# Where the additions to the residual stream stand in VectorE's queue during the gate

## The chip, the cores and the metric

The kernel runs on one core of a Trainium2 chip. The core has a matrix engine (PE, TensorE), three engines for elementwise work (DVE or VectorE, ACT or ScalarE, POOL or GpSimd), and SP (SyncE), which here only issues DMAs. Each engine works through its own queue strictly in the order in which the program was built, and waits on semaphores for what the others have to deliver. The metric is the time of one execution on the device in microseconds (us). The median of three runs of the kernel before is 2712.3 us.

## The reference

One layer of a decoder trunk with float32 inputs, 2048 positions and width 1024. The change lies wholly in the last line.

```python
h = x
a = rms_norm(h, pre_mix_g);  z = a @ w_in            # q, k, v, f, u_sg, v_sg
y = concat(rms_norm(forgetting_attention(q, k, v, f + f_bias)),
           rms_norm(chunked_spatial_gating(u_sg, v_sg, ...)))
h = h + rms_norm(y @ w_out, post_mix_g)
c = rms_norm(h, pre_ffn_g)
ff = square(relu(c @ w_ff1)) @ w_ff2
h = h + rms_norm(ff, post_ffn_g)
gate = sigmoid(h @ ple_gate_w + ple_gate_b)
return h + gate * (p @ ple_w)
```

## The kernel before, in words

The kernel goes through its stages one after the other: projection, attention and spatial gating, output projection, the first feed-forward product (FF1), the second (FF2), and the gate. Every product is computed in three float32r matmuls of split operands (lines 104 to 106, `mm3`), each 128x128 by 128x512. FF1 and FF2 use a seven-product scheme. At the end of FF2, `post` normalises the feed-forward output row by row and stores it to the DRAM tensor `yS`; the residual stream before FF lies in the DRAM tensor `hS`.

The gate works on 16 tiles of 128 positions, each in two halves of 512 columns. What belongs to one tile t:

- `load_h(t)` loads the two halves of `hS` into the tile's place and the two halves of `yS` into temporaries from a pool of three (`tmp`), and adds the one to the other on VectorE (line 1452). The sum is h of the last line of the reference. There are four places for h, used in turn: tile t + 4 takes the place of tile t, and so its load waits for the last reader of tile t.
- `turn_p(t)` and `turn_h(t)` transpose p and h on PE (lines 1459 and 1466); ACT and DVE take the result out of PSUM in two parts (lines 116 and 117, `evac_split`).
- `gate(t, mid)`: for each half, PE makes the product with `ple_w` (p2, 6 matmuls) and with `ple_gate_w` (p1, 24 matmuls). Behind the first half's matmuls PE transposes the next tile (`mid`). Then DVE adds the bias (line 1486), ACT takes the sigmoid (1487), DVE multiplies with p2 (1488), POOL adds h (1489; DVE for the last tile), and SP stores the half (1490).

`load_h(t + 2)` is called ahead of `gate(t)`. The order in which the instructions of an engine come to stand in its queue isn't that of the source: a scheduler orders them by what its own model holds ready. In the kernel before it puts the additions of line 1452 where their data are ready by that model. In the steady part of the gate this is two tiles earlier than the call: the addition for tile t + 4 stands behind the first work on tile t's own outputs.

Names in the rows and pieces below: `lr` (lr1 to lr3) are the three output buffers of the gate, `acc11`, `acc10` and `T_0` the places of h, `tmp` the loaded halves of `yS`, `pf` the eight PSUM banks, `pT`, `hT`, `B`, `w1p`, `L`, `R`, `wg` and `wh` the operands of the gate's matmuls.

Of the kernel before, what the change touches and what calls it, by code (L numbers as in the profile page):

```python
# [12 lines left out]
ALU = mybir.AluOpType  # L13
# [4 lines left out]
P = 128  # L18
# [7 lines left out]
NT = S // P  # L26
# [8 lines left out]
def trunk(ctx, tc, x, p, w_in, f_bias, sg_ln_g, sg_ln_b, sg_w, sg_b, att_out_g, sg_out_g,  # L35
# [8 lines left out]
    sc, ve, po, pe, sy = nc.scalar, nc.vector, nc.gpsimd, nc.tensor, nc.sync  # L44
# [12 lines left out]
    yS = dram.tile([S, D], F32, name="yS")  # L57
# [44 lines left out]
    def mm3(ps, l, r, first, last):  # L102

        pe.matmul(ps, l[0], r[0], start=first, stop=False)  # L104
        pe.matmul(ps, l[0], r[1], start=False, stop=False)  # L105
        pe.matmul(ps, l[1], r[0], start=False, stop=last)  # L106
# [859 lines left out]
    def w1_places(pl):  # L966

        all = pl.tile([P, 3, KC, P], F32, name="w1raw")
        return all, [all[:, e] for e in range(3)]
# [4 lines left out]
    _, w1raw = w1_places(w1q)  # L974
# [24 lines left out]
    def new_ps():  # L999
        nonlocal nps  # L1000
        nps += 1
        if pf2 is None or nps % 8 < 3:
            return pf1.tile([P, 512], F32, name="pf1")
        return pf2.tile([P, 512], F32, name="pf2")

    def new_tmp():
        return tmp.tile([P, 512], F32, name="tmp")
# [422 lines left out]
    hts, hT, hplaces = {}, [], []  # L1430
# [13 lines left out]
    def load_h(t):  # L1444

        hts[t] = hplaces[t % 4]
        for hf in range(2):
            hs = slice(hf * 512, (hf + 1) * 512)
            sy.dma_start(hts[t][hf], hS[t * P:(t + 1) * P, hs])
            y = new_tmp()  # L1450
            sy.dma_start(y, yS[t * P:(t + 1) * P, hs])
            ve.tensor_tensor(hts[t][hf], hts[t][hf], y, ALU.add)

    def turn_p(t):
        pt = LR[0][:, t % 2 * PLE:(t % 2 + 1) * PLE]
        sy.dma_start(pt, p[t * P:(t + 1) * P])
        ps = new_ps().rearrange("p (a b) -> p a b", b=P)
        for kc in range(2):
            pe.transpose(ps[:, kc], pt[:, kc * P:(kc + 1) * P], ident)
        evac_split(pTs[:, t % 2], ps[:, :2], 1.0)  # L1460

    def turn_h(t):
        for g in range(2):
            ps = new_ps().rearrange("p (a b) -> p a b", b=P)
            for kk in range(4):
                pe.transpose(ps[:, kk], hts[t][g][:, kk * P:(kk + 1) * P], ident)
            evac_split(hT[2 * (t % 2) + g].rearrange("p h (k c) -> p h k c", k=4), ps, 1.0)

    def gate(t, mid):
        pT = pTs[:, t % 2]  # L1470
        for hf in range(2):
            hs = slice(hf * 512, (hf + 1) * 512)
            p2 = new_ps()
            for kc in range(2):
                w = wple[hf][kc]
                mm3(p2, (pT[:, 0, kc], pT[:, 1, kc]), (w[:, 0], w[:, 1]), kc == 0, kc == 1)
            p1 = new_ps()
            for kc in range(KC):
                w = wgt[hf][kc]
                x = hT[2 * (t % 2) + kc // 4]  # L1480
                cs = slice(kc % 4 * P, kc % 4 * P + P)
                mm3(p1, (x[:, 0, cs], x[:, 1, cs]), (w[:, 0], w[:, 1]), kc == 0, kc == KC - 1)
            if hf == 0 and t + 1 < NT:
                mid()
            ot = LR[1 + (2 * t + hf) % 3]
            ve.tensor_tensor(ot, p1, gb[hf], ALU.add)  # L1486
            sc.activation(ot, ot, AF.Sigmoid)
            ve.tensor_tensor(ot, p2, ot, ALU.mult)  # L1488
            (ve if t == NT - 1 else po).tensor_tensor(ot, ot, hts[t][hf], ALU.add)  # L1489
            sy.dma_start(out[t * P:(t + 1) * P, hs], ot)  # L1490

    wgt = [[], []]

# [7 lines left out]
    last = len(steps2)  # L1501
    early_g = {}

    def at(i, f):
        early_g.setdefault(i, []).append(f)

    for e in range(4):
        kc, hf = e // 2, e % 2
# [25 lines left out]
    gb = []  # L1534
    at(last - 12, late_places)
    for t in range(2):
        at(last - 10 + t, lambda t=t: load_h(t))
    at(last - 17, places2)
    for e in range(6):
        at(last - 17 + 2 * e, lambda e=e: wg_in(wgpl[6 + e]))  # L1540
# [35 lines left out]
    while raws_w:  # L1576
        split_wide()
    for t in range(NT):
        if t + 2 < NT:
            load_h(t + 2)  # L1580
        def turns():
            turn_p(t + 1)
            turn_h(t + 1)

        gate(t, turns)
        for _ in range(2):
            if tail:
                tail.pop(0)()
# [25 lines left out]
```

## Time and profile before

| | |
|---|---|
| runs | 2712.3 us median of 3 (2711.87 to 2718.76) |
| the profiled execution's own time | 2715.74 us |
| its span, first to last instruction | 2714.0 us |
| PE, busy share of the span | 97% |
| DVE, ACT, POOL | 67%, 49%, 30% |
| mean granted TensorE clock | 0.987 of full speed |
| HBM traffic | 173 GB/s over the span |

How to read it: the profile is of one execution, and the times in rows are from the start of its span. A row of the timeline is an instruction with its start, its duration, its engine, line and operands, and in brackets how long its engine had been idle before it and what ended that. Neighbouring instructions of a kind are merged into one row (x2). PE's matmuls are pipelined: one that shows 0.39 us lets the next begin 0.23 us after its own start, so PE's pace is read from starts. The gate begins at about 2460 us and is the last tenth of the span.

### The profile page before, as it was taken

To read this page: it belongs to the slowest core of one execution; us is meant where nothing else is said; L and a number is where in the kernel's file an instruction comes from. 1 tells how busy PE (TensorE), PEld (TensorE's weight loads), DVE (VectorE), ACT (ScalarE), POOL (GpSimd) and SP (SyncE) were. 2 spreads that over 40 slices of the span, in tenths; PEclk is the share of its full clock that TensorE was granted. 3 is DMA by queue.
4 is the path that set the end of the run, shared out by engine and by line. 5 is a ranking of instruction groups with operands and counts; after the bars stand their busy time and mean duration, and the time that the engine had idled before them with its cause. 6 is when DMAs were issued, how large, how long until landed. Compare 5 with 4: busy or idle time off the path is not lost.

```text
span 2714.0 us, 37423 instructions
## 1 busy us (share of the span) xinstructions
PE 2620.9 (97%) x12316; PEld 2127.5 (78%) x12316; DVE 1822.2 (67%) x3212; ACT 1342.5 (49%) x2632; POOL 806.6 (30%) x695
## 2 busy tenths in 40 slices
PE   8999999999899999979999999999999999999998
PEld 7787978777677777757788788888888888888777
DVE  5547586866777655578878677678786696874333
ACT  6344433357777777655555455445435444452111
POOL 5444443410000000243444223336360262401111
PEclk8999999999999999989999999999999999999999
DMA  5565756597878776455655854448466644683331
GB/s 167 143 188 143 197 141 170 149 221 207 199 180 186 165 192 152 134 163 192 218 201 174 305 176 145 150 151 282 139 204 210 199 146 141 208 263 101 105 109 50
DMA packets 440611, 472.85 MB, mean 174 GB/s; under 512 B 155616, under 2 KB 269664, under 8 KB 440416
## 3 DMA queue, kind: packets, MB, share of 16 engines
q1 hardware_dynamic: 430179, 454.39, 56.9%
q10 hardware_dynamic: 10237, 16.07, 2.2%
q8 instruction: 97, 1.59, 0.3%
q14 instruction: 98, 0.80, 0.1%
HBM read 336.38 MB, written 133.96 MB: 173 GB/s over the span
## 4 chain that ended last, share of the span: by engine, by line
PE 46%; DMA 4%; DVE 4%; POOL 2%; issue 2%; ACT 1%; SPq 0%; DVEq 0%; POOLq 0%; ACTq 0%
PE pf L106 15%; PE pf L104 15%; PE pf L105 15%; DMA acc<-hS 2%; POOL lr L1489 1%; DMA w1raw<-in_w_ff_dram 1%; DVE lr L1486 1%; DVE lr L1488 1%; DVE w1p L994 0%; DMA px<-hS 0%; DMA T<-hS 0%; DMA B<-jS 0%; DVE ws L1170 0%; POOL hq L1197 0%; DMA cS<-px 0%
## 5 line engine op out<-in xcount | busy, mean ns | idle before, releaser
L104 PE MATMUL pf<-B,w1p 128*128 128x512 f32 x752 | 298.5, 397 | 14.8 <-ACT w1p L991 13.6
L106 PE MATMUL pf<-B,w1p 128*128 128x512 f32 x752 | 296.5, 394 | 2.8 <-DVE w1p L994 2.7
L1197 POOL TENSOR_TENSOR hq<-hq,hq 128x512 f32<-128x512 f32 x128 | 197.5, 1554 | 336.4 <-ACT hq L1191 298.7
L105 PE MATMUL pf<-B,w1p 128*128 128x512 f32 x752 | 297.3, 395 | 0.0
L660 DVE TENSOR_TENSOR hl<-pr,hl 128x512 fp32r<-128x512 f32 (+1 forms) x320 | 191.9, 608 | 104.6 <-ACT hl L659 87.9
L100 POOL TENSOR_TENSOR wsp<-wraw,wsp 128x344 fp32r<-128x344 f32 (+1 forms) x176 | 199.2, 1149 | 195.1 <-ACT wsp L96 184.6
L651 ACT ACTIVATE pr<-pS,bias 128x512 f32<-128x512 f32 (+1 forms) x320 | 196.6, 622 | 108.8 <-PE pS L647 66.2
L172 DVE TENSOR_REDUCE mx<-pM 128x1 f32<-128x512 f32 (+3 forms) x288 | 169.5, 597 | 78.4 <-PE pM L169 77.7
L104 PEld LDWEIGHTS pf<-B,w1p 128*128 128x128 f32 x752 | 141.8, 189 | 49.6 <-ACT w1p L991 14.1
L104 PE MATMUL pacc<-wsp,wide 128*128 128x344 f32 (+1 forms) x480 | 167.6, 349 | 8.8 <-ACT ug L358 5.5
L104 PE MATMUL pf<-R,L 128*128 128x512 f32 x452 | 175.9, 389 | 0.0
L105 PE MATMUL pf<-R,L 128*128 128x512 f32 x452 | 175.8, 389 | 0.0
L106 PE MATMUL pf<-R,L 128*128 128x512 f32 x452 | 175.8, 389 | 0.0
L106 PEld LDWEIGHTS pf<-B,w1p 128*128 128x128 f32 x752 | 141.6, 188 | 37.4 <-DVE w1p L994 4.3
L105 PEld LDWEIGHTS pf<-B,w1p 128*128 128x128 f32 x752 | 141.8, 189 | 31.9
L106 PE MATMUL pacc<-wsp,wide 128*128 128x344 f32 (+1 forms) x480 | 163.4, 340 | 0.5 <-DVE wide L117 0.5
L105 PE MATMUL pacc<-wsp,wide 128*128 128x344 f32 (+1 forms) x480 | 163.2, 340 | 0.0
L659 ACT CAST hl<-pr 128x512 fp32r<-128x512 f32 (+3 forms) x272 | 146.5, 549 | 8.6 <-DMA vS<-hl 2.2
L991 ACT CAST L<-lr 128x512 fp32r<-128x512 f32 x113 | 70.3, 622 | 150.1 <-PE pf L105 120.1
L994 DVE TENSOR_TENSOR w1p<-ws,w1p 128x512 fp32r<-128x512 f32 (+1 forms) x136 | 117.2, 867 | 36.7 <-ACT w1p L991 35.2
L994 DVE TENSOR_TENSOR L<-lr,L 128x512 fp32r<-128x512 f32 x113 | 96.0, 849 | 64.8 <-ACT L L991 64.6
L991 ACT CAST w1p<-w1raw 128x512 fp32r<-128x512 f32 (+1 forms) x123 | 73.4, 598 | 128.7 <-PE pf L105 121.9
(443 smaller groups left out, 7187.1 us busy)
## 6 DMA issues: line engine op xcount, KB each, us to landing
hidC<-hq SPq DMA_DIRECT2D x224, 256.0 KB
lr<-hidC SPq DMA_DIRECT2D x224, 256.0 KB
w1raw<-in_w_ff_dram SPq DMA_DIRECT2D x64, 512.0 KB
w1raw<-in_w_ff_dram SPq DMA_DIRECT2D x128, 256.0 KB
wraw<-in_w_in_dram SPq DMA_DIRECT2D x96, 256.0 KB
wraw<-in_w_in_dram SPq DMA_DIRECT2D x88, 172.0 KB
KM<-kS ACTq DMA_DIRECT2D x80, 132.0 KB
jS<-C SPq DMA_DIRECT2D x19, 512.0 KB
```

The costliest lines, as they stand in the source:

```text
L100: e.tensor_tensor(dst[:, 1], src, dst[:, 0].bitcast(F32), ALU.subtract)
L104: pe.matmul(ps, l[0], r[0], start=first, stop=False)
L105: pe.matmul(ps, l[0], r[1], start=False, stop=False)
L106: pe.matmul(ps, l[1], r[0], start=False, stop=last)
L172: ve.tensor_reduce(mx[:, tt, c:c + 1], ps[:, :full], AX.X, ALU.max)
L651: sc.activation(pr[:, off:], ps[:, off:], AF.Exp, bias=bias_of(b)[:, j, h:h + 1])
L659: sc.copy(hl[:, 0, off:], pr[:, off:])
L660: ve.tensor_tensor(hl[:, 1, off:], pr[:, off:], hl[:, 0, off:].bitcast(F32), ALU.subtract)
L991: sc.copy(dst[:, 0], src)
L994: (po if lo == "pool" else ve).tensor_tensor(dst[:, 1], src, dst[:, 0].bitcast(F32), ALU.subtract)
L1197: po.tensor_tensor(t, x, y, op)
L1486: ve.tensor_tensor(ot, p1, gb[hf], ALU.add)
```

## The change

`load_h` keeps its loads and returns a function that does the two additions. In the gate's loop this function is called behind `gate(t)`, within a block that queues what it traces on VectorE behind one given instruction: the tile's last multiplication (line 1488 before, 1492 now). Such an edge sets the order in VectorE's queue alone; nothing waits for it. For tiles 0 and 1, which are loaded during FF2, the additions follow their loads as before.

```diff
     def load_h(t):
         hts[t] = hplaces[t % 4]
+        ys = [new_tmp() for _ in range(2)]
         for hf in range(2):
             hs = slice(hf * 512, (hf + 1) * 512)
             sy.dma_start(hts[t][hf], hS[t * P:(t + 1) * P, hs])
-            y = new_tmp()
-            sy.dma_start(y, yS[t * P:(t + 1) * P, hs])
-            ve.tensor_tensor(hts[t][hf], hts[t][hf], y, ALU.add)
+            sy.dma_start(ys[hf], yS[t * P:(t + 1) * P, hs])
+
+        def add_h():
+            for hf in range(2):
+                ve.tensor_tensor(hts[t][hf], hts[t][hf], ys[hf], ALU.add)
+        return add_h
...
-            ve.tensor_tensor(ot, p2, ot, ALU.mult)
+            done = ve.tensor_tensor(ot, p2, ot, ALU.mult)
             (ve if t == NT - 1 else po).tensor_tensor(ot, ot, hts[t][hf], ALU.add)
             sy.dma_start(out[t * P:(t + 1) * P, hs], ot)
+        return done
...
-        at(last - 10 + t, lambda t=t: load_h(t))
+        at(last - 10 + t, lambda t=t: load_h(t)())
...
     for t in range(NT):
-        if t + 2 < NT:
-            load_h(t + 2)
+        add_h = load_h(t + 2) if t + 2 < NT else None
...
-        gate(t, turns)
+        done = gate(t, turns)
+        if add_h is not None:
+            with tc.issue_after(done.ins):
+                add_h()
```

The order of PE's, ACT's and POOL's instructions stays what it was. DVE's queue in the gate, before, for tile 1 (its halves go to lr3 and lr1; acc11_2 and acc11_3 are the place of tile 5):

```order
L1486 TENSOR_TENSOR lr3_15928<-pf2_22557,acc10_0_17919 128x512
L117 SCALAR_TENSOR_TENSOR pT4_17928<-pf2_22583,pT4_17928 128x256
L117 SCALAR_TENSOR_TENSOR hT0_22082<-pf2_22588,hT0_22082 128x512
L117 SCALAR_TENSOR_TENSOR hT1_22083<-pf2_22595,hT1_22083 128x512
L1488 TENSOR_TENSOR lr3_15928<-pf2_22550,lr3_15928 128x512
L1452 TENSOR_TENSOR acc11_2_17925<-acc11_2_17925,tmp_22769 128x512
L1486 TENSOR_TENSOR lr1_15926<-pf1_22614,acc10_1_17920 128x512
L1488 TENSOR_TENSOR lr1_15926<-pf1_22607,lr1_15926 128x512
L1452 TENSOR_TENSOR acc11_3_17926<-acc11_3_17926,tmp_22773 128x512
L1486 TENSOR_TENSOR lr2_15927<-pf2_22681,acc10_0_17919 128x512
```

The same place now (T_0 is the place of tile 3):

```order
L1490 TENSOR_TENSOR lr3_15928<-pf2_22555,acc10_0_17919 128x512
L117 SCALAR_TENSOR_TENSOR pT4_17928<-pf2_22581,pT4_17928 128x256
L117 SCALAR_TENSOR_TENSOR hT0_22082<-pf2_22586,hT0_22082 128x512
L117 SCALAR_TENSOR_TENSOR hT1_22083<-pf2_22593,hT1_22083 128x512
L1492 TENSOR_TENSOR lr3_15928<-pf2_22548,lr3_15928 128x512
L1490 TENSOR_TENSOR lr1_15926<-pf1_22612,acc10_1_17920 128x512
L1492 TENSOR_TENSOR lr1_15926<-pf1_22605,lr1_15926 128x512
L1455 TENSOR_TENSOR T_0_15924<-T_0_15924,tmp_22542 128x512
L1455 TENSOR_TENSOR T_0_15924<-T_0_15924,tmp_22543 128x512
L1490 TENSOR_TENSOR lr2_15927<-pf2_22679,acc10_0_17919 128x512
```

Before, one addition for the tile four ahead stood behind each half; now both additions for the tile two ahead stand behind the second half. The four additions for tiles 2 and 3 thereby leave DVE's queue in the last steps of FF2.

SP's queue before, from the store of tile 1's first half on (tmp_22875 is a half of tile 6, tmp_22973 of tile 7):

```order
L1490 DMA out_0_dram<-lr3_15928 128x512
L1449 DMA acc11_2_17925<-hS_62 128x512
L1451 DMA tmp_22875<-yS_63 128x512
L1490 DMA out_0_dram<-lr1_15926 128x512
L1449 DMA acc11_3_17926<-hS_62 128x512
L1451 DMA tmp_22973<-yS_63 128x512
```

The same place now (tmp_22667 is the second half of tile 4, tmp_22768 the first of tile 5):

```order
L1494 DMA out_0_dram<-lr3_15928 128x512
L1450 DMA acc11_2_17925<-hS_62 128x512
L1494 DMA out_0_dram<-lr1_15926 128x512
L1451 DMA tmp_22667<-yS_63 128x512
L1451 DMA tmp_22768<-yS_63 128x512
L1450 DMA acc11_3_17926<-hS_62 128x512
```

The loads of `hS` keep their place behind the stores; those of `yS` now stand in pairs behind the second half's store, and each fetches for a nearer tile.

## Rows read from the trace of the kernel before

**Rows 1.** The page's head

```profile
span 2714.0 us, 37423 instructions
```

**Rows 2.** Busy time by stretch: length, PE, PEld, DVE, ACT, POOL, clock, DMA

```profile
2420.00:2440.00 20.00, 20.00 (x90) 16.57 (x89) 15.91 (x25) 8.00 (x14) 0.65 (x1) 1.00 0.92 299
...
2467.67:2542.00 74.33, 74.33 (x351) 61.48 (x350) 26.98 (x46) 14.20 (x25) 12.15 (x10) 1.00 0.37 119
2542.00:2671.23 129.23, 123.26 (x561) 98.80 (x560) 44.51 (x74) 20.93 (x41) 21.90 (x17) 0.99 0.32 100
...
2553.40:2556.80 3.40, 3.40 (x8) 2.64 (x9) 0.54 (x1) 0.00 (x0) 1.28 (x1) 0.53 0.25 92
...
2671.23:2707.92 36.69, 36.69 (x171) 30.08 (x169) 10.74 (x17) 5.88 (x11) 5.14 (x4) 1.00 0.10 37
```

**Rows 3.** PE's waits in the gate: who, for whom, us in total, times, longest

```profile
PE pf L106 <- DVE pT L117: 5.2, 6, 1.7
PE pf L104 <- DVE lr L1488: 0.6, 1, 0.6
```

**Rows 4.** PE's timeline: start, us; the transposes of p, one row a tile

```profile
2467.67 0.38 PE L1459 MATMUL pf<-ident,lr 128*128 128x128 f32 x2
...
2542.00 0.38 PE L1459 MATMUL pf<-ident,lr 128*128 128x128 f32 x2
...
2671.23 0.38 PE L1459 MATMUL pf<-ident,lr 128*128 128x128 f32 x2
...
2686.10 0.38 PE L1459 MATMUL pf<-ident,lr 128*128 128x128 f32 x2
```

**Rows 5.** PE's timeline at its first long wait in the gate

```profile
2552.21 0.50 PE L106 MATMUL pf<-B,pT 128*128 128x512 f32 x1 [1.67 <-DVE pT L117]
...
2553.40 0.63 PE L104 MATMUL pf<-wg,hT 128*128 128x512 f32 x1
...
2556.39 0.63 PE L105 MATMUL pf<-wg,hT 128*128 128x512 f32 x1
```

**Rows 6.** DVE's waits in the gate

```profile
DVE acc L1452 <- DMA acc<-hS: 89.1, 18, 5.8
DVE T L1452 <- DMA T<-hS: 24.2, 5, 4.9
```

**Rows 7.** The chain that ended last, in order of time: start, us, what

```profile
2482.05 3.27 DMA acc<-hS
...
2488.91 1.30 POOL lr L1489
...
2490.61 3.03 DMA acc<-hS
...
2498.14 2.84 DMA acc<-hS
...
2546.50 3.93 DMA acc<-hS
...
2627.34 2.81 DMA acc<-hS
```

**Rows 8.** Line 1452's additions in the gate: ns min/median/max, first and last start

```profile
L1452 DVE TENSOR_TENSOR acc<-acc,tmp x18: 691/693/695, 2479.0 to 2647.1; 128x512 f32<-128x512 f32 x18
L1452 DVE TENSOR_TENSOR T<-T,tmp x6: 691/692/693, 2525.8 to 2662.9; 128x512 f32<-128x512 f32 x6
```

**Rows 9.** The timeline of DVE, POOL and PE in tile 13

```profile
2680.80 0.69 DVE L1488 TENSOR_TENSOR lr<-pf,lr 128x512 f32<-128x512 f32 x1 [0.70 <-ACT lr L1487]
...
2681.57 1.28 POOL L1489 TENSOR_TENSOR lr<-lr,acc 128x512 f32<-128x512 f32 x1 [5.54 <-DVE lr L1488]
...
2686.32 0.93 PE L1466 MATMUL pf<-ident,T 128*128 128x128 f32 x7
```

**Rows 10.** The timeline of POOL and DVE near the end of FF2

```profile
2421.03 0.65 POOL L993 TENSOR_SCALAR wh<-tmp 128x512 fp32r<-128x512 f32 x1 [14.83 <-DMA tmp<-in_ple_gate_w_dram]
...
2421.11 1.10 DVE L994 TENSOR_TENSOR w1p<-w1raw,w1p 128x512 fp32r<-128x512 f32 x1
```

## The prediction

> **What bounds the kernel now.** I read the busy time by stretch first, to see where PE waits at all, then the waits of PE, the chain that ended last, and the waits of DVE. The reader is to see that PE has no gap in the last steps of FF2 (20.00 of 20 us), none in the gate's first 74.33 us, and none after 2671.23, but that it misses 6 us of 129.23 between 2542.00 and 2671.23 [rows 2]. Its waits there are all for DVE: 5.2 us for the evacuation of the transposes and 0.6 us for a multiplication that frees a PSUM bank [rows 3]. DVE itself isn't short of time (44.51 of 129.23 us busy, rows 2). It stands 89.1 + 24.2 = 113.3 us before the additions of line 1452, waiting for loads of `hS` [rows 6], with the evacuations queued behind.
>
> The chain shows why. A half's addition on POOL releases the place of h; SP issues the store, then the load into that place; DVE waits for the landing, adds, and only then does the next half's bias addition, evacuation and multiplication, after which POOL can do its next addition. This closes a ring through DMA, DVE, POOL and SP that goes round once in two halves, that is one tile. From the load at 2482.05 to that at 2498.14 are 16.09 us, of which the two landings take 3.27 + 3.03 = 6.30 and the rest 9.79 [rows 7]. The 24 additions go from 2479.0 to 2662.9 [rows 8]: 183.9 us for 23 halves, 15.99 us a tile. PE needs 14.87 us for a tile when nothing holds it: 2671.23 to 2686.10, and 74.33 / 5 = 14.87 in the stretch from 2467.67 to 2542.00 [rows 4]. So DVE falls behind by 15.99 - 14.87 = 1.12 us a tile, 12.9 us in 11.5 tiles. The PSUM banks let PE run ahead for a while, which is why its first long wait comes only at 2552.21.
>
> **The change part by part.** First, what it removes. Nothing on DVE then waits for a load that was issued moments before. DVE's work in a tile is 5.4 us against 14.87 (26.98 us in five tiles, rows 2), so PE is alone on the path. What PE lost is read from starts: from 2542.00 to 2671.23 are eight tiles in 129.23 us [rows 4], against 8 x 14.87 = 118.96. That is 10.27 us, and it is the whole term. It holds the 6 us of gaps and also what follows them: after the wait that ended at 2552.21 the granted clock fell to a half, the lower of its two levels [rows 2], and eight matmuls ran 0.63 us long, starting 0.43 us apart instead of 0.23, from 2553.40 to 2556.39 [rows 5], some 1.6 us. With no wait there is no such fall: the stretch before 2542.00 was at clock 1.00 throughout [rows 2].
>
> Second, the four additions of tiles 2 and 3 leave FF2. PE doesn't wait there [rows 2], so this is worth nothing; they cost 4 x 0.69 us in the gate's first two tiles instead, where DVE has some nine idle microseconds a tile.
>
> Third, what it moves. The 28 additions stay, 0.69 us each [rows 8], two behind each tile's last multiplication. What is queued behind them is the next half's bias addition, due a half later. But the transposes of h, on PE itself, now read their result soon. The trace shows the very place where the last pair will stand: the multiplication of tile 13's second half starts at 2680.80, so at a pace of about 0.6 us behind it the two additions end near 2682.7; PE transposes tile 15 at 2686.32 [rows 9]. That leaves 3.6 us of cover in each of 14 tiles. Before, an addition stood more than two tiles ahead of its reader. I cost this at nothing; if the cover is gone, every microsecond beyond it is PE's, 14 times.
>
> The loads must be there too. `hS` for tile t + 4 is still fetched behind tile t's stores and is now read two tiles later. `yS` goes through three temporaries: the order shows the second half of tile 4 fetched at the end of tile 1 for an addition at the end of tile 2, 14.87 us on. The POOL addition of 2681.57 ends at 2682.85, the next load behind a store comes 0.40 us later (2490.21 to 2490.61), and the longest landing is 3.93 [rows 7, 9]: 2687.2 at the latest for one load, well ahead of 2696. Issuing the pair of `yS` loads now waits for the additions that free two temporaries (near 2682.7, sooner than POOL lets the store ahead of them go), and behind the pair stand only the next loads of `hS` and of p, which are read a tile or more later.
>
> A cost that the trace shows only elsewhere: the pair will run beside POOL's addition (2681.57 for 1.28 us, rows 9). At 2421.11 a DVE subtraction with both inputs in SBUF took 1.10 us beside a POOL instruction of 0.65, where such an instruction otherwise takes 0.69 [rows 8, 10], so 0.41 us were lost to an overlap of 0.57. The bounds are nothing and the full 1.28 us; the pair then ends by 2684.0, still 2.3 us early. I take no cost, since either end is covered. The Trainium skill speaks against the change here: "SBUF — State Buffer", section "Who interferes with whom", has a VectorE instruction with two SBUF inputs and a GpSimd instruction that reads SBUF exclude each other, the second waiting for the whole of the first. The trace nearly agrees (0.41 of 0.57 us). By that rule the sum stays the same, but the cover of 3.6 us shrinks to 2.3, and rival (c) below is the likelier for it.
>
> The sum: the profiled execution took 2715.74 us, its span 2714.0 [rows 1]. 2715.74 - 10.27 = 2705.5 for an execution like it. The median of the runs is 3.4 us below it, so 2712.3 - 10.3 = **2702.0 us**.
>
> **The rivals.** (a) The same mechanism is worth less. The gain hangs on the landing time: a mean landing shorter by 0.1 us takes 0.2 us from each of 11.5 tiles, 2.3 us in all. If all of the 3.4 us by which the median lies below the profiled execution came from shorter landings in the gate, the loss there would be 6.9 us and the changed kernel would take 2705.4. For it: the spread of landings, 2.81 to 3.93 us [rows 7]. Against: the runs spread by 7 us themselves, so 3.4 needs no reason. It counts as no change from 2704.2 on.
>
> (b) No gain: PE isn't held by the ring when nobody profiles, or another wait takes its place. The ring loses to PE's pace at landings below (14.87 - 9.79) / 2 = 2.54 us, and the mean landing would have to be better than the trace's best, 2.81. The time would be about 2712. The Trainium skill, "DMA: Bandwidth & Descriptors", section "Anatomy of one DMA — SWDGE (gpsimd) path", gives a fit for transfers issued from GpSimd, about 2.0 us fixed plus the bytes at 436 GB/s; the estimate for 256 KB would be 2.6 us, and by it the ring would hardly hold PE and the change give nothing. No landing of the trace is that short, and the measurement decides.
>
> (c) Slower: the pair itself becomes late. If it had to wait for a load issued behind the store of the same tile (2682.85 + 0.40) and landing after 3.93 us, at 2687.2, it would end at 2688.5, and PE's transposes be 2.2 us late in 14 tiles: 30 us, so 2732, and the clock may fall on top. It decides from 10.3 / 14 = 0.73 us of lateness a tile, that is with the additions ending over 4.4 us later than worked out. For it: the cover falls from more than two tiles to 3.6 us, and POOL may eat 1.3 of that. Against: the order of SP has each load a whole tile ahead.
>
> **How the numbers follow.** A measurement of this kernel tells about 0.3%, 8.1 us, from no change, so the forecast lies just beyond that bound. The forecast (gain above 8.1 us) has 0.70, (a) 0.20, (b) 0.06, (c) 0.04. Faster 0.70, within the bound 0.26, slower 0.04. The forecast's own range is 2698.5 to 2704.2; the lower end is a gain of 14, the ring's whole 12.9 and a fall of the clock more. The range for 8 in 10 takes in (a): 2698.5 to 2708.
>
> **What would show it.** In the changed profile: tiles at 14.87 us from 2467.67 on, with the transposes of tile 15 near 2675.8 instead of 2686.10; no PE wait for lines 117 or 1492 in the gate; DVE's 113.3 us of waiting for `hS` gone, and its bias additions waiting for PE instead; clock 1.00 from 2467 to PE's end; the additions ending over 2 us before the transposes. It is wrong if the tiles stay at 16 us (the waits for loads have come back elsewhere), if PE waits for the additions at the transposes of h, or if the gate is as forecast and the time was lost in another stage.

## The result, and the profile after

The changed kernel took 2701.47 us (median of five runs, 2696.39 to 2704.53), the kernel before beside it 2713.57 (five runs, 2711.87 to 2718.76). The ratio is 0.9943, with a 95% interval of 0.9926 to 0.996. The difference of the means is 13.8 us, that of the medians 12.1. The interval stands for a gain of some 10.9 to 20.1 us, so five runs of each tell the size only roughly. The forecast was 2702.0 us by a gain of 10.3, which as a ratio is 0.9962, just outside the interval. A second comparison of the same two programs gave 0.9959. (One execution of the kernel before, in a later comparison, took 5217 us and is left out of every ratio and mean here.)

The profiled execution after took 2701.87 us. First the stretches, in the columns of [rows 2]:

```profile
2467.67:2542.00 74.33, 74.33 (x351) 61.48 (x350) 35.63 (x50) 13.49 (x26) 14.85 (x11) 1.00 0.40 124
2542.00:2656.00 114.00, 114.00 (x535) 94.17 (x534) 50.14 (x67) 18.88 (x36) 23.52 (x16) 1.00 0.34 110
2656.00:2694.00 38.00, 38.00 (x177) 31.12 (x175) 13.03 (x19) 5.88 (x11) 5.52 (x4) 1.00 0.14 43
```

PE is busy for the whole of each, where it missed 6 us of the middle one before, and the granted clock stays at 1.00. The list of PE's waits between 2440 and 2701 us, which held two rows before [rows 3], is now empty. The 32 transposes of p, two a tile, give the whole gate in one row of each kernel. Before:

```profile
L1459 PE MATMUL pf<-ident,lr x32: 270/271/272, 2454.1 to 2686.2; 128*128 128x128 f32 x32
```

And after:

```profile
L1463 PE MATMUL pf<-ident,lr x32: 270/271/272, 2450.5 to 2672.3; 128*128 128x128 f32 x32
```

From the first to the last were 232.1 us and are now 221.8, so the gate gives 10.3 us. (All lengths below called "the gate" are taken from these two starts.) The last transposition stands 27.8 us from the span's end in both. The other 3.6 us of this pair of executions lie ahead of the gate: it begins at 2454.1 in the one and at 2450.5 in the other.

DVE's waits, in the columns of [rows 6]:

```profile
DVE lr L1490 <- issue: 99.8, 27, 4.8
DVE lr L1490 <- PE pf L106: 13.5, 4, 4.9
```

Its 113.3 us before the additions, for loads of `hS`, are gone. It now stands idle before the bias additions. The profile names PE as the releaser of four of these and none ("issue") for 27, but their starts follow PE's products: the one at 2650.65 begins 0.09 us after the end of the last matmul that it reads (2650.17 + 0.39). The pair of additions of one tile, with the multiplication ahead of it and POOL's addition beside it, on the timeline of DVE, POOL and PE (to be read against [rows 9]):

```profile
2666.91 0.69 DVE L1492 TENSOR_TENSOR lr<-pf,lr 128x512 f32<-128x512 f32 x1 [0.70 <-ACT lr L1491]
2667.51 2.38 DVE L1455 TENSOR_TENSOR T<-T,tmp 128x512 f32<-128x512 f32 x2
...
2667.68 1.67 POOL L1493 TENSOR_TENSOR lr<-lr,acc 128x512 f32<-128x512 f32 x1 [5.55 <-DVE lr L1492]
...
2672.42 1.04 PE L1470 MATMUL pf<-ident,T 128*128 128x128 f32 x8
```

The pair ends at 2669.89, 2.53 us ahead of the transposition that reads it. The two additions took 2.38 us, and 1.29 where they run beside no POOL instruction (below, the kernel with four more instructions). POOL's addition took 1.67, and 1.28 undisturbed [rows 9]. Taken singly, the first addition of the pair lasted 0.68 us (from 2667.51), as an undisturbed one does, and the second 1.78 (from 2668.11).

### The profile page after: what moved, and what is told of

Its sections match the earlier page's. It is cut to its first block, busy times and chain, and to the rows that moved or that the text cites. A ratio compares the mean times of both kernels' runs of the same rounds, so it can differ in the third digit from the quotient of the medians.

```text
span 2700.1 us, 37436 instructions
## 1 busy us (share of the span) xinstructions
PE 2613.7 (97%) x12316; PEld 2123.4 (79%) x12316; DVE 1841.5 (68%) x3212; ACT 1342.4 (50%) x2632; POOL 811.5 (30%) x695
## 4 chain that ended last, share of the span: by engine, by line
PE 53%; DMA 2%; DVE 1%; issue 1%; ACT 1%; POOL 0%; SPq 0%; DVEq 0%; ACTq 0%; POOLq 0%
PE pf L106 17%; PE pf L104 17%; PE pf L105 17%; PE pf L1470 1%; DMA w1raw<-in_w_ff_dram 0%; DMA px<-hS 0%; DMA cS<-px 0%; DVE w1p L994 0%; DMA B<-jS 0%; PE pf L1018 0%; DVE ws L1170 0%; DVE hq L1189 0%; DVE z L748 0%; POOL tmp L1068 0%; DMA ysT<-ysS 0%
## 5 line engine op out<-in xcount | busy, mean ns | idle before, releaser
L104 PE MATMUL pf<-B,w1p 128*128 128x512 f32 x752 | 298.3, 397 | 14.4 <-ACT w1p L991 13.6
```

## The experiments

Three questions: is the change worth the gate's 10.3 us or more, is the ring of loads what held PE, and how much cover does the late pair have?

**The two kernels again.** Both unchanged.

> The kernel before, unchanged, measured against itself. Gate-alone theory (the change is worth the 10.3 us by which PE's eight late tiles fell behind, everything ahead of the gate differs by chance): ratio 1.000, in a band of about 0.002 to either side; in its profile the stretch from the first to the last transpose of p is again near 232 us (222 would be no loss), while the time of the first transpose (2454.1 in the first profile) moves by 2 to 5 us from execution to execution. Landing theory (executions of before lose more in the gate than the profiled one): the stretch is 235 us or more. Earlier-stages theory (the change also gains 3.6 us ahead of the gate): the first transpose again at 2454 within 1 us.

> The changed kernel once more, in five further rounds. Gate-alone theory: ratio about 0.9962 (10.3 of 2713 us), so the first result of 0.9943 was low by chance; stretch from first to last transpose of p 221.8 us, first transpose anywhere from 2449 to 2456. Landing theory and earlier-stages theory: ratio again about 0.994 to 0.995, and by the latter the first transpose again near 2450.5.

The kernel before against itself gave 1.000 (0.9989 to 1.0011), with a gate of 232.4 us (2455.2 to 2687.6); the changed kernel gave 2704.45 us and 0.9959 (0.9943 to 0.9975). The difference of the means is now 11.3 us. The changed kernel's row:

```profile
L1463 PE MATMUL pf<-ident,lr x32: 270/270/271, 2460.8 to 2682.5; 128*128 128x128 f32 x32
```

The gate is 221.7 us again, but it begins 10.3 us later than in the first profile of the very same program, and outside the 2449 to 2456 that was expected. So the stages ahead scatter from execution to execution by as much as the change is worth, and a profile pair alone can't split a gain of 13.8 us.

**The early pairs left in FF2.** The changed kernel, but the additions for tiles 2 and 3 follow their loads as before.

```diff
         add_h = load_h(t + 2) if t + 2 < NT else None
+        if t < 2:
+            add_h()
+            add_h = None
```

> The changed kernel, but the additions for tiles 2 and 3 stay in the last steps of FF2 as before; only those for tiles 4 to 15 stand behind the last multiplication. Gate-alone theory: same as the change, 221.8 us from first to last transpose of p, no PE wait, ratio near 0.996. Earlier-stages theory: the part gained ahead of the gate is lost again, first transpose near 2454 and ratio about 0.0013 above that of the changed kernel run beside it.

2706.77 us, ratio 0.9964 (0.9951 to 0.9978), the gate at 221.8 us without a PE wait. By the means the gain is 11.2 us, against 11.3 for the changed kernel beside it. The four additions that left FF2 are worth nothing that shows.

**A shorter ring, the additions where they were.** The kernel before, with the final addition of every half on VectorE instead of GpSimd.

```diff
-            (ve if t == NT - 1 else po).tensor_tensor(ot, ot, hts[t][hf], ALU.add)
+            ve.tensor_tensor(ot, ot, hts[t][hf], ALU.add)
```

> The kernel before with its additions to the residual stream where they were, but the last addition of each half on VectorE instead of GpSimd for all tiles: the ring loses two GpSimd additions of 1.30 us and their hand-overs for two of about 0.7, so it goes from 15.99 to about 14.7 us a tile, just below PE's 14.87. Ring theory: DVE still waits some 5 us for each load of hS, yet PE's waits nearly vanish (under 2 us instead of 10.3 lost), stretch 222 to 224 us, ratio near 0.997. If DVE's waits as such were what cost the time (any wait in front of the evacuation), PE would still lose about 10 us and the ratio be 1.000.

2700.8 us, ratio 0.9940 (0.9927 to 0.9952), more than the 0.997 expected; the gate took 221.8 us (2452.4 to 2674.2) where 222 to 224 were expected, with no PE wait. DVE still waits for `hS`, 87.2 us in 24 waits:

```profile
DVE acc L1452 <- DMA acc<-hS: 65.4, 18, 4.1
DVE T L1452 <- DMA T<-hS: 21.8, 6, 4.1
```

The queue still blocks on a load 24 times, and it costs PE nothing. So it isn't the waiting as such that cost the 10.3 us. It is that the ring went round in 15.99 us where PE needs 14.87.

**The ring made longer, first attempt.** The kernel before with a GpSimd copy of each output half onto itself between the final addition and the store.

```diff
             (ve if t == NT - 1 else po).tensor_tensor(ot, ot, hts[t][hf], ALU.add)
+            if t < NT - 1:
+                po.tensor_scalar(ot, ot, 1.0, 0.0, ALU.mult, ALU.add)
             sy.dma_start(out[t * P:(t + 1) * P, hs], ot)
```

> The kernel before with one more GpSimd instruction (a copy of the output half onto itself) between the final addition of each half and its store, so only the ring is made longer: by one GpSimd instruction a half. The nearest row for such an instruction is 0.65 us on GpSimd, so the ring of 15.99 us a tile grows by 2 x 0.65 = 1.3 us, to 17.3; up to 2 x 1.28 if the copy costs as much as the addition. Ring theory (the rate at which the additions get their loads sets the gate): the loss against 14.87 us a tile grows from 1.12 to 2.4 us, some 28 us over 11.5 tiles of which the first 2.6 are covered as before; the stretch from the first to the last transposition of p grows from 232.1 to about 247 us (up to 262), ratio to the kernel before about 1.0055 (up to 1.011). Theory that PE's own evacuations are the limit and the ring only a symptom: the copy is off PE's path, the stretch stays at 232, ratio 1.000.

It came out faster: 2705.49 us, ratio 0.9947 (0.9935 to 0.996), the gate at 221.7 us with no PE wait. The expectation was wrong about what the edit does. The copy only delays the store, and the load that refills h's place doesn't need the store: the scheduler moved it ahead, in all 24 of these loads. The timeline of POOL, SP and DVE in three halves of this kernel:

```profile
2561.98 1.29 POOL L1489 TENSOR_TENSOR lr<-lr,acc 128x512 f32<-128x512 f32 x1 [5.51 <-DVE lr L1488]
...
2566.38 0.69 DVE L1452 TENSOR_TENSOR acc<-acc,tmp 128x512 f32<-128x512 f32 x1 [4.48 <-DMA acc<-hS]
...
2569.15 1.28 POOL L1489 TENSOR_TENSOR lr<-lr,acc 128x512 f32<-128x512 f32 x1 [5.17 <-DVE lr L1488]
...
2573.34 0.69 DVE L1452 TENSOR_TENSOR acc<-acc,tmp 128x512 f32<-128x512 f32 x1 [4.28 <-DMA acc<-hS]
...
2576.84 1.29 POOL L1489 TENSOR_TENSOR lr<-lr,T 128x512 f32<-128x512 f32 x1 [5.71 <-DVE lr L1488]
...
2578.16 0.32 SPq L1449 DMA_DIRECT2D T<-hS  x1
2578.87 0.34 SPq L1492 DMA_DIRECT2D out_dram<-lr  x1
...
2580.81 0.69 DVE L1452 TENSOR_TENSOR T<-T,tmp 128x512 f32<-128x512 f32 x1 [4.05 <-DMA T<-hS]
```

And the chain that ended last in the kernel before, in the same stretch:

```profile
2561.42 1.29 POOL lr L1489
2562.73 0.34 SPq L1490
2563.12 2.85 DMA acc<-hS
...
2569.56 1.30 POOL lr L1489
2570.87 0.34 SPq L1490
2571.21 0.33 issue
2571.54 2.98 DMA acc<-hS
...
2577.38 1.30 POOL lr L1489
2578.70 0.34 SPq L1490
2579.09 3.40 DMA acc<-hS
```

From the end of POOL's addition to DVE's start are 3.11, 2.91 and 2.68 us here (as 2580.81 - 2578.13). In the kernel before, from POOL's end to the landing are 3.26, 3.66 and 3.81 us (as 2579.09 + 3.40 - 2578.68). The mean difference is 0.68 us a half, 1.4 a tile, against the 1.12 by which the ring was too long. So the run shortened the ring by accident, and speaks for the ring by the opposite of what it was to show.

**The ring made longer, held in place.** The kernel before again, with the load pinned behind the store, the addition pinned behind the half's multiplication, the evacuations and the next bias addition pinned behind it, and the copy ahead of the final addition, where both the load and the store wait for it. (`load_half`, cut here, loads one half and makes its addition.)

```diff
+                with after(pin.get("add")):
+                    mid()
...
+            with after(pin.pop("add", None)):
+                ve.tensor_tensor(ot, p1, gb[hf], ALU.add)
...
+            mult = ve.tensor_tensor(ot, p2, ot, ALU.mult)
+            if t < NT - 1:
+                po.tensor_scalar(ot, ot, 1.0, 0.0, ALU.mult, ALU.add)
             (ve if t == NT - 1 else po).tensor_tensor(ot, ot, hts[t][hf], ALU.add)
+            store = sy.dma_start(out[t * P:(t + 1) * P, hs], ot)
+            if t + 4 < NT:
+                pin["add"] = load_half(t + 4, hf, mult, store)
```

> The kernel before with its ring held in place and made longer. Each half's addition for the tile four ahead is recorded behind that half's store, its load pinned behind the store on SyncE as in the kernel before, and its place on VectorE pinned directly behind the multiplication, with the evacuations and the next bias addition behind it; and a GpSimd copy of 0.62 us (as measured in the run with the copy ahead of the store) stands between multiplication and final addition. The ring of 15.99 us a tile grows by 2 x (0.62 + 0.1) us, and by up to 0.7 us more as the second half's Sigmoid is no longer covered by the evacuations: 17.4 to 18.1 us. Ring theory: the loss against 14.87 us is 2.6 to 3.2 us a tile over some 11.5 tiles, less the 2.6 us that PE's running ahead covers: 27 to 35 us; the stretch from the first to the last transposition of p takes 249 to 257 us instead of 232.1, the ratio to the kernel before is 1.006 to 1.009, more if PE's clock falls in the waits. Theory that the ring isn't what sets the kernel's gate, or that the scheduler's order of it was a symptom: the stretch stays at 232, ratio 1.000.

2746.21 us, ratio 1.0098 (1.0073 to 1.0124). The additions and the transposes of p in this kernel:

```profile
L1457 DVE TENSOR_TENSOR acc<-acc,tmp x18: 691/693/694, 2480.5 to 2674.8; 128x512 f32<-128x512 f32 x18
L1457 DVE TENSOR_TENSOR T<-T,tmp x6: 691/693/695, 2535.4 to 2693.9; 128x512 f32<-128x512 f32 x6
...
L1474 PE MATMUL pf<-ident,lr x32: 270/271/274, 2454.8 to 2716.2; 128*128 128x128 f32 x32
```

The ring now takes 213.4 / 11.5 = 18.56 us a tile and the gate 261.4. The size was outside the expectation (17.4 to 18.1 us a tile, 249 to 257 us, and a ratio of 1.006 to 1.009), the ring being half a microsecond longer than worked out, but the mechanism is there at nearly four times the size: (18.56 - 14.87) x 11.5 = 42.4 us, less the microseconds by which PE had run ahead, against 39.6 measured. PE's waits are again for DVE alone: 12.8 us for the evacuations of the transposes and 13.9 us for bias additions and multiplications that free PSUM banks. No run has the pinned order without the copy, so how the 2.57 us that the ring grew by are shared between the two isn't shown.

**Three more profiles of the kernel before.** What else the first 13.8 us could hold: a gate that loses more in other executions.

> The kernel before, unchanged, one more profile. Seven kernels whose gate ran at PE's own pace (221.8 us from the first to the last transposition of p) were 11.2 to 16.4 us faster than the kernel before by the means of their runs, 13.6 on average, while the two profiles of the kernel before show 232.1 and 232.4 us there, a loss of 10.3 to 10.6. Theory of the varying gate (landings differ from execution to execution, and most executions lose more than these two): some of the looks show 234 to 238 us. Theory of the gate as seen: every look shows 231.5 to 233.5, and what is left of the 13.6 lies ahead of the gate, where the first transposition comes at 2447 to 2461 us in the profiles of all kernels.

> As the look before it: 231.5 to 233.5 us from the first to the last transposition of p if the gate's loss is the same in every execution, 234 to 238 in some if it varies.

> As the two looks before it: 231.5 to 233.5 us from the first to the last transposition of p if the gate's loss is the same in every execution, 234 to 238 in some if it varies.

The gate's loss does vary: the three gave 232.2, 234.0 and 234.3 us, and the last two lie outside the band for a gate that is always the same. But the loss stays below the 13.6 us of the comparisons in all of them. The third of the three profiles:

```profile
L1452 DVE TENSOR_TENSOR acc<-acc,tmp x18: 691/693/695, 2472.7 to 2643.1; 128x512 f32<-128x512 f32 x18
L1452 DVE TENSOR_TENSOR T<-T,tmp x6: 691/692/693, 2520.6 to 2658.7; 128x512 f32<-128x512 f32 x6
...
L1459 PE MATMUL pf<-ident,lr x32: 270/272/274, 2447.7 to 2682.0; 128*128 128x128 f32 x32
```

All profiles in which the ring holds PE, from rows like these (the ring is the time from the first of the 24 additions to the last, over 11.5 tiles; the loss is the gate less 221.8):

| | ring, us a tile | gate | loss | 11.5 x (ring - 14.87) less the loss | gate begins |
|---|---|---|---|---|---|
| before, first profile | 15.99 | 232.1 | 10.3 | 2.6 | 2454.1 |
| before, again | 16.03 | 232.4 | 10.6 | 2.8 | 2455.2 |
| third profile | 16.02 | 232.2 | 10.4 | 2.8 | 2454.7 |
| fourth profile | 16.17 | 234.0 | 12.2 | 2.8 | 2454.2 |
| fifth profile | 16.17 | 234.3 | 12.5 | 2.5 | 2447.7 |
| ring held and made longer | 18.56 | 261.4 | 39.6 | 2.8 | 2454.8 |

The fifth column is what PE had run ahead by, and it is the same 2.5 to 2.8 us in all six: one rule gives every length. (The ring and the gate are two measures of one stretch that DVE and PE go through together, so the table shows by how much PE ran ahead; that the ring is the cause rests on the kernels that change it.) The loss of the kernel before is 10.3 to 12.5 us, 11.2 on average. The fifth profile took 2711.51 us in all, less than the other four, and lost the most in the gate; it was short because its gate began at 2447.7.

What makes the ring longer in the last two profiles of the kernel before is the landings. On the timelines of SP and DVE, the 24 loads of `hS` took on average 3.24, 3.25 and 3.24 us from their issue to DVE's addition in the first three profiles, and 3.32 us in the last two. Those 0.08 us, twice a tile, are the 0.16 us by which the ring went from some 16.01 to 16.17, and over 11.5 tiles 1.8 of the 1.9 us by which the loss grew.

**The changed kernel with a longer final step.** The GpSimd copy of the first attempt, put into the changed kernel.

> The changed kernel with the same extra GpSimd instruction per half. Ring theory (the change took the loads' ring off PE's path, so its length no longer matters): the stretch from the first to the last transposition stays at 221.8 us, ratio to the kernel before 0.9962, as for the changed kernel. Rival (the ring is only shorter than PE now and comes back when it is made 1.3 to 2.6 us a tile longer): the stretch grows by 10 us or more, ratio 1.000 or above. The run is also a third look at the size of the change: the theory that only the gate gains (10.3 to 10.6 us) expects 0.996, the theory that stages ahead of the gate gain too expects 0.9945 or less.

2700.97 us, ratio 0.9945 (0.9928 to 0.9961); the gate at 221.8 us, no PE wait. This edit didn't lengthen the loads' ring either: as in the first attempt, the load stands ahead of the store, and is issued when POOL's addition ends, beside the copy (load at 2542.32, addition to 2542.29, copy from 2542.38, store at 2543.03). So the rival, that a longer ring comes back in the changed kernel, wasn't tested. What the run adds is one more comparison with a gate at PE's pace: the difference of the means is 15.9 us, with a gate no better than the one that gave 11.3.

**The pair made late.** Two more kernels, made from the changed one: a number n of VectorE instructions on a scratch tile stands ahead of the pair; the next half's bias addition stays behind the pair, and a tile's second-half products behind the transposes.

```diff
+            for _ in range(n):
+                with tc.issue_after(done.ins):
+                    done = ve.tensor_tensor(junk, junk, junk, ALU.max)
             with tc.issue_after(done.ins):
-                add_h()
+                behind = add_h().ins
```

Four of them:

> The changed kernel with four VectorE instructions on a scratch tile between the last multiplication of a tile and the pair of additions, some 0.6 to 0.7 us each: the pair comes 2.4 to 2.8 us later. The changed kernel's trace has the pair ending 2.53 us ahead of the transposition of h (2669.89 against 2672.42), and in 2.38 us instead of 1.29 as it runs beside the GpSimd addition. Cover theory: the delayed pair runs behind the GpSimd addition, takes 1.3 us instead of 2.38 and ends 1.3 to 1.7 us later, still ahead of the transposition by 0.8 us or more; the stretch stays at 221.8 us, ratio 0.996. Rival (no cover beyond what was measured, and the pair stays slow): 0 to 0.3 us late in 14 tiles, 0 to 4 us, ratio 0.996 to 0.9975.

2707.23 us, ratio 0.996 (0.9948 to 0.9972), the gate at 221.9 us and no PE wait. DVE and PE in one tile:

```profile
2658.01 3.84 DVE L1600 TENSOR_TENSOR junk<-junk 128x512 f32<-128x512 f32 x4
2661.76 1.29 DVE L1456 TENSOR_TENSOR acc<-acc,tmp 128x512 f32<-128x512 f32 x2
...
2662.92 1.04 PE L1472 MATMUL pf<-ident,acc 128*128 128x128 f32 x8
```

The pair, now past POOL's addition, takes 1.29 us, and the four instructions ahead take 3.84 as one of them meets POOL in its place. The pair ends at 2663.05, when PE is already at the first half's transposes (the expectation had it 0.8 us or more ahead of them), and still nothing is lost, because the second half's come half a microsecond later. Ten of them:

> The same with ten such instructions, 6.0 to 6.9 us: the pair begins near 2673.6 to 2674.5 on the scale of the changed kernel's tile 13 and ends 1.3 us later, 2.5 to 3.4 us behind the transposition's old start. Theory of the prediction's slower rival (once the cover is gone every microsecond is PE's, 14 times): 35 to 48 us more than the changed kernel, ratio about 1.009 to 1.014, and up to 1.02 if PE's clock falls after each wait. Rival (PE makes up for it because the second half's products can be done first or run ahead in PSUM): under 10 us, ratio below 1.000. In this kernel the products of a tile's second half stand behind the transpositions on PE in all tiles.

2787.54 us, ratio 1.0249 (1.0229 to 1.0269), the gate 296.7 us, 74.9 more. PE's waits in the gate (who, for whom, us in total, times, longest):

```profile
PE pf L1472 <- DVE acc L1456: 36.7, 10, 5.4
PE pf L1472 <- DVE T L1456: 16.3, 4, 4.1
PE pf L106 <- DVE pT L117: 1.3, 2, 0.8
PE pf L104 <- ACT pT L116: 1.3, 2, 0.8
```

Fourteen tiles wait for the additions, 53.0 us in all, 3.8 each. And the stretches behind one such wait, in the columns of [rows 2]:

```profile
2605.00:2612.00 7.00, 3.55 (x17) 2.64 (x15) 6.76 (x11) 0.38 (x1) 0.32 (x1) 1.00 0.31 95
2612.60:2614.50 1.90, 1.87 (x9) 1.90 (x10) 1.14 (x3) 0.60 (x1) 0.00 (x0) 0.50 0.45 130
2614.50:2618.00 3.50, 3.50 (x14) 2.81 (x13) 1.93 (x3) 1.12 (x2) 1.29 (x1) 0.78 0.24 84
2618.00:2628.90 10.90, 10.90 (x49) 8.84 (x48) 5.81 (x8) 0.63 (x1) 1.67 (x1) 1.00 0.30 95
```

When PE starts again after some 4 us of waiting, the granted clock is 0.50, the lower level, and it is back at 1.00 in the last stretch. The gate grew by 74.9 us and the waits come to 55.6; the other 19.3 are 1.4 us for each of the 14 waits, which fits the clock's fall (estimated at 1.6 us a fall in the prediction). So the slower rival is a real place: once the cover is gone each microsecond is PE's, in every tile, with the clock on top. The expectation's 35 to 48 us without the clock was too low, since the ten instructions came to over 8 us, not 6.0 to 6.9: the evacuation of p stands among them and the first meets POOL.

## Why the prediction was nearly right, and where it missed

**The mechanism was right.** The kernel before was held in the gate by the ring of loads through DVE. Taking it away gave 14.87 us a tile to the end, no PE wait, clock 1.00 and the transposes of tile 15 at 2672.21, which is 2675.8 as forecast less the 3.6 us by which the gate began earlier. The shortened rings (two kernels with the additions where they were, gate 221.8 and 221.7) and the lengthened one (261.4) show the ring as the cause from both sides. That the four additions which left FF2 don't matter is shown by the kernel that kept them there. The other part of the change, the new order of the loads of `yS`, wasn't run by itself; PE has no wait in the gate with it.

**The step that failed is the size of the one term.** The prediction took the 10.27 us of one profiled execution as the loss of any ("That is 10.27 us, and it is the whole term"). Five profiles of the kernel before show 10.3 to 12.5 us, and the one it used is the smallest. The mean, 11.2, is a ratio of 0.9959, the value that the second comparison gave and within the interval of the first. Rival (a) had the reason for it, the landing time, and its price (2.3 us for 0.1 us a landing, against 1.9 for 0.08), but with the wrong sign: it reckoned with landings shorter than those of the one profile, and nothing in the prediction reckoned with longer ones. It read the 3.4 us between the profiled execution and the median as possibly the gate's. The fifth profile shows the reverse, the shortest of the five executions with the largest loss. What makes executions differ most is the time ahead of the gate.

That the time itself came out within 0.5 us of the forecast (2701.47 against 2702.0) is in part luck: the kernel before beside it had a median of 2713.57 and not 2712.3, and the difference of the medians, 12.1 us, was larger than the forecast gain by about as much.

**The scatter ahead of the gate was left out of the range for the gain.** The gate begins at 2447.7 to 2455.2 us in five profiles of the kernel before, and at 2447.5 to 2460.8 in seven of kernels whose gate takes 221.7 to 221.9. Their means are 2453.2 and 2453.1, so the profiles show no gain ahead of the gate. The difference has arisen by 1498 us, where the last transposes of FF1's input start at 1485.0 to 1497.9; from there to the gate these twelve profiles need 961.2 to 964.4. Single comparisons of kernels with the same gate gave 11.2 to 16.4 us, and of the first one's 13.8 us, 11.2 are explained by the gate. The lower end of the forecast's range, a gain of 14, had room for a larger loss in the gate, but none for this scatter.

**What stays open.** The seven comparisons of kernels with a gate of 221.7 to 221.9 us average 13.6 us, which is 2.4 above the mean loss in the gate. The profiled executions alone differ by just the gate's 11.2 (2715.7 us on average for the five of the kernel before, 2704.5 for the seven). The 54 executions of the kernel before in these comparisons and profiles average 2717.3 us, the 40 of the seven kernels 2704.1. So the rest lies mostly in executions of the kernel before that weren't profiled. That may be chance (the seven scatter by 2.2 us, each has five or six runs, and six of them share two sets of runs of the kernel before), or those executions may lose a little more in the gate. The runs don't tell these apart; no profile shows a second place.

**The cover.** Forecast 3.6 us, or 2.3 if the pair had to give way to POOL for the whole 1.28; measured 2.53, near the lower end. The pair was lengthened by 1.09 us and POOL's addition by 0.39. The Trainium skill, "SBUF — State Buffer", section "Who interferes with whom", has such a VectorE instruction with two SBUF inputs and a GpSimd instruction that reads SBUF share one read interface as an exclusive lock. One after the other the three would take 1.29 + 1.28 = 2.57 us; together they took 2.38, so the trace nearly agrees. The single times look like taking turns: the first addition isn't lengthened at all (0.68 us), POOL's, which starts 0.51 us before the first ends, takes 0.39 longer, and the second, which starts 1.24 us before POOL's ends, takes 1.09 longer. The value taken for the sum, nothing, holds: 2.53 us was enough, and even a pair that ended 2.66 us later (2663.05 against transposes from 2662.92) cost nothing.

**Rivals (b) and (c)** didn't come about. What (c) gave as its price, every microsecond beyond the cover 14 times, is what the kernel with ten more instructions paid.

## What to carry to other kernels

An in-order queue that waits for a load issued moments before isn't a loss in itself. Follow the ring that the load closes (release, store, load, landing, addition, next release) and compare its period with the bound engine's: here 15.99 to 16.17 against 14.87 us cost 10.3 to 12.5 us, and each of three ways to shorten or open the ring (the addition moved out, a faster final addition, the load ahead of the store) gave all of it back in the gate and no more. When the gain is about as large as the scatter between executions, read it from the stage in several profiles, not from one profile or one comparison.

## What the runs showed of the hardware that was not expected

In the kernel whose loads of `hS` (256 KB each) were issued ahead of a store of 256 KB, DVE used them on average 2.85 us after their issue (24 loads, 2.55 to 3.81; as 2578.16 to 2580.81). Behind the store, in the first profile of the kernel before, it was 3.24 us (24 loads, 2.90 to 4.03). That the store in flight slows the load is a guess from this; it wasn't measured by itself.

Two additions on DVE and one on POOL with all inputs in SBUF, side by side, took 2.38 us where the pair alone took 1.29 and POOL's addition alone 1.28: nearly as long as one after the other.

After waits of PE of 3.8 us on average, the gate lost a further 1.4 us for each wait; behind the one shown the granted clock was 0.50, the lower level, and then rose back to 1.00.
